# A two-layer hybrid trunk on one core: chunked linear attention with two-chunk scores, its steps placed by hand between projection matmuls

## The chip, the core and the metric

The kernel runs on one core of a Trainium2 chip. TensorE (PE in the profile) does the matmuls and writes PSUM, 8 banks of 128 partitions by 512 float32; VectorE (DVE), ScalarE (ACT) and GpSimd (POOL) do the rest, each in the order of its own instruction stream, and wait for one another by semaphores. DMA engines bring the weights. The metric is the device time of one execution, in microseconds (us). The kernel before took 851.46 us, the median of 3 runs (850.23 to 853.15).

## The reference

512 tokens of width 1024 go through two layers and a last RMSNorm. Each layer does a modulated RMSNorm, one input projection, two mixers side by side, a product with SiLU of a gate, an output projection and a gated residual. The change lies in the second layer, whose mixers are chunked gated linear attention (4 heads, keys of 128, values of 256, chunks of 64 tokens) and stick-breaking attention (8 heads of 128).

```python
def gla(q, k, v, log_a):
    ...
    bcum = jnp.cumsum(la, axis=2)
    b_last = bcum[:, :, -1]
    q_dec = qf * jnp.exp(bcum)
    k_inv = kf * jnp.exp(-bcum)
    k_end = kf * jnp.exp(b_last[:, :, None] - bcum)
    att = jnp.einsum('bnthk,bnshk->bnhts', q_dec, k_inv)
    att = jnp.where(mask, att, 0.0)
    o_intra = jnp.einsum('bnhts,bnshv->bnthv', att, vf)

    def step(state, xs):
        qd, ke, vc, bl = xs
        o = jnp.einsum('bthk,bhkv->bthv', qd, state)
        state = jnp.exp(bl)[..., None] * state + jnp.einsum('bshk,bshv->bhkv', ke, vc)
        return state, o
```

The outputs of a head are then normalised over their 256 values. Stick-breaking attention takes q, k and v of its own from the same projection.

## The kernel before

Everything is float32. A projection is exact to nearly float32: a weight tile is split into a high part (`whi`, ScalarE, L184) and the rest (`wlo`, VectorE, L185), both in the type fp32r, and three matmuls add up high by high, low by high and high by low (`mm3`, L198 to L200). `c_unit` makes 256 output channels for all 512 tokens in two PSUM banks; `t_unit` makes 512 channels with the tokens on the partitions, in four. These use 6 banks of the tag `mm`; everything small shares 2 banks of the tag `aux`. One weight tile feeds 24 projection matmuls and comes by one DMA of 512 KB on SyncE's queue; there are 4 buffers for raw tiles and 3 for split ones.

Of the second layer the order of the source is: the values of the linear attention (`gv`, two `t_unit`), the low-rank gate (`glr`, 16 matmuls, L564 and L565), and then for each of two pairs of heads `c`: `decay` of both heads (one matmul over 32 rows, L572, then logs, eight scans and exponentials on ScalarE and VectorE), the projections of k and q with their evacuation into decayed copies (`k_evac`, `q_evac`), and four steps `p`, each over two chunks of 64 (128 tokens). A step has four parts for both heads: scores (L638 and L639), output (L652 and L654), transposes of the decayed k (L661) and state update (L667, L671). For the scores the two chunks need different decays, so the first chunk is one matmul of 64 keys by 64 queries with `k1` (L638), and the second is one of 128 keys by 64 queries with `k2` (L639). ScalarE (L643) and VectorE (L644) copy them to `att`, and GpSimd (L645) puts zeros above the diagonal. After four steps come the norms (L684 and L685), then the two value projections `sv` of the stick-breaking attention, and then its 8 heads.

In this whole part a scheduler sets the order of each engine's instructions, TensorE's too. It is free to put small matmuls between any two projection matmuls. Only the stick-breaking heads stand under `manual_schedule`: there TensorE's order is that of the source, and `boundary`, called after each 12 projection matmuls (`quarter`), issues what `steps` holds for that gap (L715, L742 and L750).

Of the kernel before, what the change touches and what calls it, by code (L numbers as in the profile page):

```python
# [9 lines left out]
F32 = mybir.dt.float32  # L10
# [7 lines left out]
P = 128  # L18
# [21 lines left out]
def pack_inputs(i):  # L40
# [57 lines left out]
def trunk(ctx: ExitStack, tc: tile.TileContext, d, out):  # L98
# [447 lines left out]
    gv = [big("gv") for _ in range(TB)]  # L546
    t_unit(lambda kp: nxt(), 4, h_left(), tok_evac(gv, 0),
# [14 lines left out]
    ps = bank("aux")  # L562
    for k in range(KT):
        T.matmul(ps, gwv[:, k, :], h_hi[k], start=k == 0, stop=False)  # L564
        T.matmul(ps, gwv[:, k, :], h_lo[k], start=False, stop=k == KT - 1)  # L565
    glr = slot("silu")
    A.copy(out=glr[0:32], in_=ps[0:32])
# [27 lines left out]
    t_unit(lambda kp: nxt(), 4, h_left(), tok_evac(gv, 1))  # L595
# [5 lines left out]
    for c in range(2):  # L601
        dec = [decay(2 * c + j) for j in range(2)]
        k1, k2, k3, qd, qi = ([None, None] for _ in range(5))
# [29 lines left out]
        for p in range(TB):  # L633
# [14 lines left out]
            for j in range(2):  # L648
                for vt in range(2):
# [3 lines left out]
                    if p:  # L653
                        T.matmul(ov, st[j][:, vt * P:(vt + 1) * P], qi[j][:, r], start=False, stop=True)  # L654
# [208 lines left out]
```

## Time and profile before

| | |
|---|---|
| median of 3 runs | 851.46 us (850.23 to 853.15) |
| the profiled execution | 850.56 us |
| its span, first to last instruction | 848.8 us |
| busy: TensorE, VectorE, ScalarE, GpSimd | 97%, 60%, 47%, 8% of the span |
| mean granted TensorE clock | 0.995 of full speed |
| HBM read | 105.56 MB, 127 GB/s over the span |

The time of an execution is its span and some 2 us around it. Busy shares are averages over stages. A group of small float32 matmuls counts two records for each instruction. TensorE's records overlap, since a matmul drains while the next one streams, so the price of an instruction is the distance from its start to the next one's start and not its duration.

### The profile page before, as it was taken

The numbers are of one execution on the slowest core, as the hardware profiler recorded it, in microseconds if no ns is written. First come the engines' busy times: TensorE is split into PE (matmuls) and PEld (weight loads), VectorE is DVE, ScalarE is ACT, GpSimd is POOL, SyncE is SP. The second block draws the span as 40 slices with busy tenths as digits, with TensorE's granted clock in tenths as the row PEclk, the third lists the DMA queues.
The fourth block names the chain that finished last, engine by engine and source line by source line (L and its number), as shares of the span: only waits on it lengthen the run. The fifth ranks groups of instructions, "written<-read, shape, count | busy, mean of one in ns | idle before, by whom it ended". The sixth has DMA issues, their size and how long they took to land.

```text
span 848.8 us, 10038 instructions
## 1 busy us (share of the span) xinstructions
PE 825.2 (97%) x3720; PEld 661.3 (78%) x3720; DVE 511.0 (60%) x813; ACT 396.3 (47%) x663; POOL 65.8 (8%) x135
## 2 busy tenths in 40 slices
PE   5999999999999999999999999999999999989996
PEld 3778888888888887787877778877777777768884
DVE  6866655597773477642735643275657668433875
ACT  5463221233333366542425343365757678433553
POOL 2002111100000000000010200011010101020011
PEclk9999999999999999999999999999999999999998
DMA  8886555554552245423211202322121213232362
GB/s 287 291 293 220 178 170 174 199 178 160 180 181 89 84 151 187 133 78 100 98 51 50 75 29 96 100 82 92 61 89 46 83 47 100 79 95 87 115 218 78
DMA packets 31362, 108.31 MB, mean 128 GB/s; under 512 B 3633, under 2 KB 3761, under 8 KB 31314
## 3 DMA queue, kind: packets, MB, share of 16 engines
q1 hardware_dynamic: 30738, 106.63, 38.0%
q10 hardware_dynamic: 576, 1.05, 0.3%
q8 instruction: 29, 0.48, 0.2%
q14 instruction: 19, 0.16, 0.1%
HBM read 105.56 MB, written 2.10 MB: 127 GB/s over the span
## 4 chain that ended last, share of the span: by engine, by line
PE 88%; DVE 4%; DMA 3%; issue 1%; ACT 1%; POOL 1%; SPq 0%; POOLq 0%; ACTq 0%; DVEq 0%
PE mm L199 25%; PE mm L200 25%; PE mm L198 25%; PE aux L715 2%; PE aux L750 2%; DMA raw<-in_adaT 1%; DVE wlo L185 1%; PE aux L742 1%; DMA raw<-in_w 1%; DVE raw L174 1%; PE aux L652 1%; PE aux L464 1%; DMA x<-in_x 1%; PE aux L667 1%; PE aux L639 1%
## 5 line engine op out<-in xcount | busy, mean ns | idle before, releaser
L185 DVE TENSOR_TENSOR wlo<-raw,whi 128x1024 fp32r<-128x1024 f32 (+1 forms) x146 | 177.5, 1217 | 124.7 <-ACT whi L184 124.6
L184 ACT ACTIVATE whi<-raw 128x1024 fp32r<-128x1024 f32 (+1 forms) x146 | 152.6, 1045 | 195.2 <-PE mm L199 84.4
L198 PE MATMUL mm<-hhi,whi 128*128 128x512 f32 x576 | 233.1, 405 | 0.0
L200 PE MATMUL mm<-hhi,wlo 128*128 128x512 f32 x576 | 225.6, 392 | 0.0
L199 PE MATMUL mm<-hlo,whi 128*128 128x512 f32 x576 | 224.7, 390 | 0.0
L199 PEld LDWEIGHTS mm<-hlo,whi 128*128 128x128 f32 x576 | 108.3, 188 | 24.0 <-issue 2.7
L200 PEld LDWEIGHTS mm<-hhi,wlo 128*128 128x128 f32 x576 | 108.1, 188 | 23.7 <-issue 0.8
L198 PEld LDWEIGHTS mm<-hhi,whi 128*128 128x128 f32 x576 | 108.3, 188 | 23.2 <-issue 1.9
L174 DVE CUSTOM_DVE_ANT_0 raw<-raw,sc,cols 128x1024 f32<-128x1024 f32 x48 | 61.5, 1283 | 50.6 <-DMA raw<-in_adaT 50.5
L198 PE MATMUL mm<-whi,hhi 128*128 128x512 f32 x192 | 76.4, 400 | 0.4 <-ACT whi L184 0.2
L199 PE MATMUL mm<-wlo,hhi 128*128 128x512 f32 x192 | 76.4, 398 | 0.1
L200 PE MATMUL mm<-whi,hlo 128*128 128x512 f32 x192 | 74.7, 396 | 0.8 <-DVE hlo L319 0.8
L200 PE MATMUL mm<-whi,r 128*128 128x512 f32 x160 | 62.6, 391 | 0.0
L198 PE MATMUL mm<-whi,r 128*128 128x512 f32 x160 | 62.4, 391 | 0.0
L199 PE MATMUL mm<-wlo,r 128*128 128x512 f32 x160 | 62.4, 390 | 0.0
L200 PEld LDWEIGHTS mm<-whi,hlo 128*128 128x128 f32 x192 | 36.3, 189 | 8.8 <-DVE hlo L319 1.7
L198 PEld LDWEIGHTS mm<-whi,hhi 128*128 128x128 f32 x192 | 36.5, 191 | 8.3 <-ACT whi L184 0.6
L199 PEld LDWEIGHTS mm<-wlo,hhi 128*128 128x128 f32 x192 | 36.7, 191 | 7.8 <-DVE wlo L185 0.5
L190 DVE TENSOR_TENSOR r<-y,r 128x256 fp32r<-128x256 f32 (+1 forms) x60 | 29.1, 509 | 19.3 <-PE mm L199 16.1
L189 ACT ACTIVATE r<-y 128x256 fp32r<-128x256 f32 (+1 forms) x60 | 27.0, 479 | 29.2 <-PE mm L200 23.2
L199 PEld LDWEIGHTS mm<-wlo,r 128*128 128x128 f32 x160 | 30.0, 188 | 6.4 <-DVE wlo L185 0.3
L198 PEld LDWEIGHTS mm<-whi,r 128*128 128x128 f32 x160 | 30.0, 188 | 6.1
(186 smaller groups left out, 1043.9 us busy)
## 6 DMA issues: line engine op xcount, KB each, us to landing
raw<-in_w SPq DMA_DIRECT2D x90, 512.0 KB, 3.3
raw<-in_adaT SPq DMA_DIRECT2D x48, 512.0 KB, 4.1
raw<-in_wo SPq DMA_DIRECT2D x48, 512.0 KB, 3.3
raw<-in_wfirst SPq DMA_DIRECT2D x8, 384.0 KB, 4.3
x<-in_x SPq DMA_DIRECT2D x4, 512.0 KB, 5.2
kq<-in_poolw SPq DMA_DIRECT2D x4, 256.0 KB, 4.4
out<-x SPq DMA_DIRECT2D x4, 256.0 KB, 2.3
out<-x ACTq DMA_DIRECT2D x4, 256.0 KB, 2.6
```

Of the source, the lines that this page charges most:

```text
L174: V.tensor_tensor_reduce(out=t, in0=t, in1=sc, scale=1.0, scalar=cols[:, C_AB[l] + b:C_AB[l] + b + 1], op0=ALU.mult, op1=ALU.add, accum_ou ...
L184: A.activation(out=hi[:, :w], in_=t[:, :w], func=AF.Copy)
L185: V.tensor_tensor(out=lo[:, :w], in0=t[:, :w], in1=hi.bitcast(F32)[:, :w], op=ALU.subtract)
L189: A.activation(out=hi, in_=src, func=AF.Copy)
L190: V.tensor_tensor(out=lo, in0=src, in1=hi.bitcast(F32), op=ALU.subtract)
L198: T.matmul(o, lh, rh, start=start, stop=False)
L199: T.matmul(o, lh, rl, start=False, stop=False)
L200: T.matmul(o, ll, rh, start=False, stop=stop)
L464: T.matmul(ps[:, t * P:(t + 1) * P], v[t][:, hd * P:(hd + 1) * P], sguw[hd // 4][:, c], start=True, stop=True)
L639: T.matmul(ps[:, j * P + 64:(j + 1) * P], k2[j][:, r], qd[j][:, rb], start=True, stop=True)
L715: T.matmul(ps[:, c0:c0 + (t + 1) * P], q[:, t * P:(t + 1) * P], k[:, :(t + 1) * P], start=True, stop=True)
L750: T.matmul(ps[:, s * P:], sv[s][:, hd * P:(hd + 1) * P], wt[s], start=s == 0, stop=s == 3)
```

## The change

The scores of a step become one matmul for each head: 128 keys of both chunks by 192 columns, which are the queries of the first chunk, those of the second, and those of the second once more with the first chunk's decay in them. So `q_evac` writes a tile `qx` of 4 times 192 columns (GpSimd's copy L624 is gone), `k_evac` makes `k1` and `k3` from whole rows and no `k2`, and the transposes of k move into the same step as the scores. Of the 192 columns the copies to `att` take the first and third 64 for the first chunk's keys and the second 64 for the second chunk's keys.

TensorE's order is fixed from the second half of `gv` on. `at` and `boundary` now serve the linear attention too: `low_rank`, the four `decay`, and, for each pair of heads, the parts `scores`, `outputs` and `norm` are given gaps between 12 projection matmuls (`plan`, `decay_at`). Each pair of heads gets one of the two `sv` projections, whose gaps take its steps: the stream of weight tiles `w1` is now gv, gv, then k, q, sv for each pair. `nxt.deepen(1)`, which splits weight tiles one ahead, starts there. `gv` and `sv` are kept as halves, the first half of `sv` in slots of the tag `y`, and `kt` has two buffers.

```diff
     g1 = 5136
     s1 = [t_tiles(w1, 1024), t_tiles(w1, 1536)]
     for c in range(2):
-        s1 += [c_tiles(w1, 512 + 256 * c), c_tiles(w1, 256 * c)]
-    s1 += [t_tiles(w1, 4112), t_tiles(w1, 4624)]
+        s1 += [c_tiles(w1, 512 + 256 * c), c_tiles(w1, 256 * c), t_tiles(w1, 4112 + 512 * c)]
     for c in range(4):
         s1 += [c_tiles(w1, 2064 + 256 * c), c_tiles(w1, 3088 + 256 * c), c_tiles(w1, g1 + 256 * c)]
     s1 += [c_tiles(w1, g1 + 256 * c) for c in range(4, 8)]
...
     glr = slot("silu")
-    A.copy(out=glr[0:32], in_=ps[0:32])
+
+    def low_rank():
+        ps = bank("aux")
+        for k in range(KT):
+            T.matmul(ps, gwv[:, k, :], h_hi[k], start=k == 0, stop=False)
+            T.matmul(ps, gwv[:, k, :], h_lo[k], start=False, stop=k == KT - 1)
+        A.copy(out=glr[0:32], in_=ps[0:32])
...
+
+
+    steps, gap = {}, [0]
+
+    def at(g, f):
+        steps.setdefault(g, []).append(f)
+
+    def boundary():
+        for f in steps.pop(gap[0], []):
+            f()
+        gap[0] += 1
+
+    def c_steps(f):
+        c_unit(nxt, f, quarter=boundary)
+        boundary()
+
+    def t_steps(dst):
+        t_unit(lambda kp: nxt(), 4, h_left(), half_evac(dst),
+               groups=[e for kp in range(4) for e in (((0, 1), (kp,)), boundary, ((2, 3), (kp,)), boundary)])
+
...
+    def gla_pair(c):
+
+        k1, k3, qx, edec, st = ([None, None] for _ in range(5))
+        o, att, kt = [], {}, {}
 
         def k_evac(j, ps):
-            e, ei, kf = (half(t) for t in dec[j])
-            k1[j], k2[j], k3[j] = slot("kq"), slot("kq"), slot("kq")
-            a, b, z, q = half(k1[j]), half(k2[j]), half(k3[j]), half(ps)
-            V.tensor_tensor(out=a[:, :, 0], in0=q[:, :, 0], in1=ei[:, :, 0], op=ALU.mult)
-            V.tensor_tensor(out=z[:, :, 1], in0=q[:, :, 1], in1=kf[:, :, 1], op=ALU.mult)
-            V.tensor_tensor(out=b[:, :, 0], in0=q[:, :, 0], in1=kf[:, :, 0], op=ALU.mult)
-            V.tensor_tensor(out=b[:, :, 1], in0=q[:, :, 1], in1=ei[:, :, 1], op=ALU.mult)
-            V.tensor_tensor(out=z[:, :, 0], in0=b[:, :, 0], in1=e[:, :, 1, 63:64].to_broadcast([P, 4, 64]),
-                            op=ALU.mult)
-        c_unit(nxt, k_evac)
-        edec = [None, None]
+            e, ei, kf = dec[2 * c + j]
+            k1[j], k3[j] = slot("kq"), slot("kq")
+            V.tensor_tensor(out=k1[j], in0=ps, in1=ei, op=ALU.mult)
+            V.tensor_tensor(out=k3[j], in0=ps, in1=kf, op=ALU.mult)
+            z = half(k3[j])[:, :, 0]
+            V.tensor_tensor(out=z, in0=z, in1=half(e)[:, :, 1, 63:64].to_broadcast([P, 4, 64]), op=ALU.mult)
 
         def q_evac(j, ps):
-            e = half(dec[j][0])
-            qd[j], qi[j] = slot("r"), slot("r")
-            V.scalar_tensor_tensor(out=qd[j], in0=ps, scalar=GLA_DK ** -0.5, in1=dec[j][0], op0=ALU.mult,
+
+            e = half(dec[2 * c + j][0])
+            qx[j] = pool.tile([P, 768], F32, name=nm("qx"), tag="qx", bufs=2)
+            x = qx[j].rearrange("p (n b c) -> p n b c", b=3, c=64)
+            V.scalar_tensor_tensor(out=x[:, :, 0:2], in0=half(ps), scalar=GLA_DK ** -0.5, in1=e, op0=ALU.mult,
                                    op1=ALU.mult)
-            a, b = half(qd[j]), half(qi[j])
-            G.tensor_copy(out=b[:, :, 0], in_=a[:, :, 0])
-            V.tensor_tensor(out=b[:, :, 1], in0=a[:, :, 1], in1=e[:, :, 0, 63:64].to_broadcast([P, 4, 64]),
+            V.tensor_tensor(out=x[:, :, 2], in0=x[:, :, 1], in1=e[:, :, 0, 63:64].to_broadcast([P, 4, 64]),
                             op=ALU.mult)
             edec[j] = sm("edec", 4)
             V.tensor_tensor(out=edec[j], in0=e[:, :, 0, 63], in1=e[:, :, 1, 63], op=ALU.mult)
-        c_unit(nxt, q_evac)
-
-        o = [slot("y") for _ in range(4)]
-        st = [None, None]
-        for p in range(TB):
+
+        def scores(p):
             r = slice(p * P, (p + 1) * P)
             ps = bank("aux")
             for j in range(2):
-                ra, rb = slice(p * P, p * P + 64), slice(p * P + 64, (p + 1) * P)
-                T.matmul(ps[0:64, j * P:j * P + 64], k1[j][:, ra], qd[j][:, ra], start=True, stop=True)
-                T.matmul(ps[:, j * P + 64:(j + 1) * P], k2[j][:, r], qd[j][:, rb], start=True, stop=True)
-            att = atts[p % 2]
-            av = att.rearrange("p (j q) -> p j q", j=2)
-            pv = ps[:, :2 * P].rearrange("p (j q) -> p j q", j=2)
-            A.copy(out=av[0:64, :, 0:64], in_=pv[0:64, :, 0:64])
-            V.tensor_copy(out=av[:, :, 64:128], in_=pv[:, :, 64:128])
-            G.affine_select(out=att, in_=att, pattern=[[0, 2], [1, P]], compare_op=ALU.is_ge, fill=0.0, base=0,
+                T.matmul(ps[:, j * 192:(j + 1) * 192], k1[j][:, r], qx[j][:, p * 192:(p + 1) * 192], start=True,
+                         stop=True)
+            att[p] = atts[p % 2]
+            av = att[p].rearrange("p (j b c) -> p j b c", j=2, c=64)
+            pv = ps[:, :384].rearrange("p (j n c) -> p j n c", j=2, c=64)
+            A.copy(out=av[0:64], in_=pv[0:64, :, 0:3:2])
+            V.tensor_copy(out=av[64:128, :, 1], in_=pv[64:128, :, 1])
+            G.affine_select(out=att[p], in_=att[p], pattern=[[0, 2], [1, P]], compare_op=ALU.is_ge, fill=0.0, base=0,
                             channel_multiplier=-1)
+            if p == TB - 1:
+                return
             ps = bank("aux")
             for j in range(2):
+                T.transpose(ps[:, j * P:(j + 1) * P], k3[j][:, r], ident)
+            kt[p] = pool.tile([P, 2 * P], F32, name=nm("kt"), tag="kt", bufs=2)
+            V.tensor_copy(out=kt[p], in_=ps[:, :2 * P])
+
...
+        def plan(g):
+            for n, f, a in ((1, scores, 0), (2, scores, 1), (3, outputs, 0), (4, scores, 2), (5, outputs, 1),
+                            (6, scores, 3), (7, outputs, 2), (9, outputs, 3), (11, norm, 0), (14, norm, 1)):
+                at(g + n, lambda f=f, a=a: f(a))
+        return k_evac, q_evac, plan
+
+    def decay_at(g, hd):
+        def f():
+            dec[hd] = decay(hd)
+        at(g, f)
+
+    nxt.deepen(1)
+    order = ctx.enter_context(ExitStack())
+    order.enter_context(tc.manual_schedule(engines={T.engine}))
+    at(0, low_rank)
+    for hd, g in enumerate((3, 5, 14, 16)):
+        decay_at(g, hd)
+    gv[1] = halves("gv")
+    t_steps(gv[1])
+    sv = [None, None]
+    for c in range(2):
+        k_evac, q_evac, plan = gla_pair(c)
+        c_steps(k_evac)
+        c_steps(q_evac)
+        plan(gap[0])
+        sv[c] = halves("sv") if c else [slot("y") for _ in range(TB)]
+        t_steps(sv[c])
```

Left out are the evacuation of `gv` and `sv` into halves, `outputs`, `squares` and `norm`, which hold the same operations as before, and the loops of the stick-breaking heads, which call the same units at the same gaps.

Where TensorE's instructions stand, in the first pair of heads, third step. Before, the scores of that step follow the state update of the step before (L667), and six projection matmuls later comes the output that needs them (`aux_3485`):

```order
L667 MATMUL aux_3470<-gv_2860,kt_3468 128x256 x2
L638 MATMUL aux_3477<-r_3397,kq_3319 64x64
L639 MATMUL aux_3477<-r_3397,kq_3320 128x64
L638 MATMUL aux_3477<-r_3404,kq_3327 64x64
L639 MATMUL aux_3477<-r_3404,kq_3328 128x64
L200 MATMUL mm_3614<-hhi_121,wlo_3618 128x512
L198 MATMUL mm_3613<-hhi_122,whi_3647 128x512
L199 MATMUL mm_3613<-hlo_130,whi_3647 128x512
L200 MATMUL mm_3613<-hhi_122,wlo_3648 128x512
L198 MATMUL mm_3613<-hhi_123,whi_3647 128x512
L199 MATMUL mm_3613<-hlo_131,whi_3647 128x512
L652 MATMUL aux_3485<-att_3203,gv_2861 128x128
```

After, the same step's scores (`qx` is the tile of queries, `aux_3587` the scores) stand alone between 12 projection matmuls and 12 more, with the transposes of k behind them:

```order
L199 MATMUL mm_3439<-whi_3510,hlo_131 128x512
L660 MATMUL aux_3587<-qx_3424,kq_3327 128x192
L660 MATMUL aux_3587<-qx_3429,kq_3332 128x192
L673 MATMUL aux_3593<-ident,kq_3328 128x128
L673 MATMUL aux_3593<-ident,kq_3333 128x128
L197 MATMUL mm_3440<-whi_3510,hhi_122 128x512
L198 MATMUL mm_3440<-wlo_3511,hhi_122 128x512
```

The output that needs these scores stands 36 projection matmuls further on, behind the output and state update of the second step and the scores of the fourth; the state update has moved directly behind the output of its own step.

On VectorE, between the evacuation of the first pair's q and its part of the first scores. Before there is one weight split (`wlo`) between them:

```order
L621 SCALAR_TENSOR_TENSOR r_3397<-mm_3335,z_3225 128x512
L625 TENSOR_TENSOR r_3398<-r_3397,z_3225 128x4x64
L621 SCALAR_TENSOR_TENSOR r_3404<-mm_3336,z_3250 128x512
L625 TENSOR_TENSOR r_3405<-r_3404,z_3250 128x4x64
L185 TENSOR_TENSOR wlo_3696<-raw_3693,whi_3695 128x1024
L644 COPY att_3203<-aux_3415 128x2x64
```

After, the decays of the second pair of heads (L586, L589, L593 and L599; `misc_3391` is the first, `misc_3464` the second) stand among them, and the copy of the transposed k (`kt`) and the score copy (`att`) come behind these rows:

```order
L651 TENSOR_TENSOR qx_3424<-qx_3424,z_3169 128x4x64
L586 TENSOR_SCALAR misc_3391<-aux_3387,cols 128x512
L589 TENSOR_TENSOR misc_3391<-misc_3391,misc_3389 128x512
L593 SCALAR_TENSOR_TENSOR misc_3396<-ones,misc_3391 128x64 x8
L649 SCALAR_TENSOR_TENSOR qx_3429<-mm_3338,z_3224 128x4x128
L599 TENSOR_TENSOR sp_3407<-misc_3396 128x512
L651 TENSOR_TENSOR qx_3429<-qx_3429,z_3224 128x4x64
L184 TENSOR_TENSOR wlo_3511<-raw_3508,whi_3510 128x1024
L654 TENSOR_TENSOR edec_3872<-z_3405 128x4
L586 TENSOR_SCALAR misc_3464<-aux_3460,cols 128x512
L589 TENSOR_TENSOR misc_3464<-misc_3464,misc_3462 128x512
L593 SCALAR_TENSOR_TENSOR misc_3469<-ones,misc_3464 128x64 x8
```

The rows show that VectorE now has two decays to do between the end of the q projection and its part of the first scores, where it had none.

## Rows read from the trace of the kernel before

**Rows 1.** The page: busy time, share of the span and instruction records of each engine (part 1), and the share of each engine in the chain of work that ended last (part 4).

```profile
PE 825.2 (97%) x3720; PEld 661.3 (78%) x3720; DVE 511.0 (60%) x813; ACT 396.3 (47%) x663; POOL 65.8 (8%) x135
...
PE 88%; DVE 4%; DMA 3%; issue 1%; ACT 1%; POOL 1%; SPq 0%; POOLq 0%; ACTq 0%; DVEq 0%
```

**Rows 2.** Five stretches of the span (us from its start), with the busy time and the number of records of each engine in it, then TensorE's granted clock, the share of the DMA engines and GB/s. The first three hold the gated linear attention, the fourth the value projection of the stick-breaking attention, the fifth the stick-breaking attention up to its last projections.

```profile
424.00:450.00 26.00, 25.32 (x150) 19.80 (x149) 8.43 (x17) 5.47 (x18) 3.21 (x5) 1.00 0.15 48
450.00:476.00 26.00, 26.00 (x108) 19.11 (x108) 20.31 (x48) 17.35 (x30) 1.36 (x2) 1.00 0.12 41
476.00:500.00 24.00, 23.77 (x142) 18.86 (x142) 9.37 (x18) 5.35 (x18) 3.85 (x5) 1.00 0.20 66
500.00:552.10 52.10, 52.10 (x232) 42.60 (x231) 18.94 (x21) 20.09 (x31) 0.00 (x0) 1.00 0.28 91
552.10:742.00 189.90, 189.90 (x849) 149.54 (x848) 123.20 (x175) 128.00 (x222) 18.15 (x48) 1.00 0.23 75
```

**Rows 3.** The waits of TensorE from 375 to 553 us: who waited for whom, us in total, times, longest.

```profile
PE aux L652 <- POOL att L645: 0.9, 2, 0.7
```

**Rows 4.** TensorE's timeline in the first pair of heads, third chunk pair: start, us, engine, line, tiles, shapes, count of records. A plain float32 matmul leaves two records, an fp32r one leaves one; the durations overlap, so a cost is read from one start to the next. L667 is the state update, L638 and L639 are the scores, L652 begins the output, L198 to L200 are projection matmuls.

```profile
437.19 1.11 PE L667 MATMUL aux<-gv,kt 128*128 128x256 f32 x4
438.23 0.33 PE L638 MATMUL aux<-r,kq 128*64 128x64 f32 x2
438.49 0.43 PE L639 MATMUL aux<-r,kq 128*128 128x64 f32 x2
438.85 0.33 PE L638 MATMUL aux<-r,kq 128*64 128x64 f32 x2
439.11 0.43 PE L639 MATMUL aux<-r,kq 128*128 128x64 f32 x2
439.35 0.48 PE L200 MATMUL mm<-hhi,wlo 128*128 128x512 f32 x1
439.67 0.39 PE L198 MATMUL mm<-hhi,whi 128*128 128x512 f32 x1
...
440.59 0.40 PE L199 MATMUL mm<-hlo,whi 128*128 128x512 f32 x1
441.67 0.49 PE L652 MATMUL aux<-att,gv 128*128 128x128 f32 x2 [0.68 <-POOL att L645]
```

**Rows 5.** The chain that ended last, 434 to 442 us: start, us that the piece adds to the chain, what.

```profile
435.09 0.22 PE aux L652 x2
...
437.35 0.95 PE aux L667 x4
...
439.64 0.27 ACT att L643
...
439.93 0.30 DVE att L644
...
440.29 1.34 POOL att L645
```

**Rows 6.** TensorE's timeline in the stick-breaking attention, around one float32 score matmul of 256 moving columns (L715) between projection matmuls.

```profile
558.99 0.39 PE L200 MATMUL mm<-hhi,wlo 128*128 128x512 f32 x1
559.22 0.59 PE L715 MATMUL aux<-kq,kq 128*128 128x256 f32 x2
559.46 0.59 PE L198 MATMUL mm<-hhi,whi 128*128 128x512 f32 x1
559.88 0.40 PE L199 MATMUL mm<-hlo,whi 128*128 128x512 f32 x1
```

**Rows 7.** Groups of TensorE instructions from 375 to 553 us: line, tiles, shapes, count of records, then busy us and mean ns of one.

```profile
L639 PE MATMUL aux<-r,kq 128*128 128x64 f32 x32 | 6.9, 296 | 0.0
...
L638 PE MATMUL aux<-r,kq 128*64 128x64 f32 x32 | 5.3, 246 | 0.0
```

**Rows 8.** VectorE's timeline in the second pair of heads: L580, L584 (eight scans) and L590 belong to one decay, L577 to the next one, L621 is the evacuation of q, L613 a product over half the columns, L185 the split of a weight tile, L644 its part of the score copy.

```profile
464.11 0.68 DVE L580 TENSOR_TENSOR misc<-misc,misc 128x512 f32<-128x512 f32 x1
464.83 1.57 DVE L584 TENSOR_TENSOR_SCAN misc<-ones,misc 128x64 f32<-128x64 f32 x8
466.43 0.69 DVE L590 TENSOR_TENSOR sp<-misc 128x512 f32<-128x512 f32 x1
467.04 0.74 DVE L577 TENSOR_SCALAR misc<-aux,cols 128x512 f32<-128x512 f32 x1
...
468.03 0.68 DVE L621 SCALAR_TENSOR_TENSOR r<-mm,z 128x512 f32<-128x512 f32 x1
...
472.42 0.41 DVE L613 TENSOR_TENSOR kq<-kq,z 128x256 f32<-128x256 f32 x1
...
475.50 1.21 DVE L185 TENSOR_TENSOR wlo<-raw,whi 128x1024 fp32r<-128x1024 f32 x1
...
477.44 0.29 DVE L644 COPY att<-aux 128x128 f32<-128x128 f32 x1 [0.41 <-ACT att L643]
```

**Rows 9.** TensorE's timeline around one decay matmul (L572, 32 rows by 512 columns).

```profile
458.29 1.12 PE L572 MATMUL aux<-silu,silu 32*128 32x512 f32 x2
459.34 0.50 PE L199 MATMUL mm<-hlo,whi 128*128 128x512 f32 x1
```

**Rows 10.** The timeline of all engines: the split of the first weight tile of `gv`'s second half, and the first matmul of the low-rank gate (L564).

```profile
371.50 1.23 DVE L185 TENSOR_TENSOR wlo<-raw,whi 128x1024 fp32r<-128x1024 f32 x1 [1.78 <-ACT whi L184]
...
375.65 0.39 PE L564 MATMUL aux<-hhi,glr_w 128*128 128x512 f32 x1
```

More of the change, by code (lines that the diff above doesn't have):

```diff
@@ L545, in trunk, with halves, half_evac @@
     nxt = stream(d["w1"])
-    gv = [big("gv") for _ in range(TB)]
-    t_unit(lambda kp: nxt(), 4, h_left(), tok_evac(gv, 0),
+    def halves(n):
+        t = [big(n) for _ in range(2)]
+        return [t[i // 2][:, (i % 2) * 512:(i % 2 + 1) * 512] for i in range(TB)]
+    def half_evac(dst):
+        return lambda t, ps: (V.tensor_copy if t % 2 else A.copy)(out=dst[t], in_=ps)
+    gv = [halves("gv"), None]
+    t_unit(lambda kp: nxt(), 4, h_left(), half_evac(gv[0]),
            groups=(late, ((0, 1), (0, 1, 2)), ((2, 3), (0, 1, 2)), ((0, 1, 2, 3), (3,))))
@@ L649, in trunk, with outputs @@
+            V.tensor_copy(out=kt[p], in_=ps[:, :2 * P])
+        def outputs(p):
+            if not p:
+                o.extend(slot("y") for _ in range(4))
+            r = slice(p * P, (p + 1) * P)
+            ps = bank("aux")
+            for j in range(2):
+                x = qx[j].rearrange("p (n b c) -> p n b c", b=3, c=64)[:, p, 0:3:2]
                 for vt in range(2):
                     c0 = j * 256 + vt * P
-                    ov = ps[:, (2 * j + vt) * P:(2 * j + vt + 1) * P]
@@ L657, in trunk @@
             if p == TB - 1:
-                break
+                squares(0)
+                return
             ps = bank("aux")
             for j in range(2):
-                T.transpose(ps[:, j * P:(j + 1) * P], k3[j][:, r], ident)
-            kt = pool.tile([P, 2 * P], F32, name=nm("kt"), tag="kt", bufs=1)
-            V.tensor_copy(out=kt, in_=ps[:, :2 * P])
-            ps = bank("aux")
-            for j in range(2):
-                c0 = j * 256
-                T.matmul(ps[:, c0:c0 + 256], kt[:, j * P:(j + 1) * P], gv[p][:, 512 * c + c0:512 * c + c0 + 256], start=True, stop=True)
+                c0 = slice(j * 256, (j + 1) * 256)
+                T.matmul(ps[:, c0], kt[p][:, j * P:(j + 1) * P], gv[c][p][:, c0], start=True, stop=True)
             for j in range(2):
@@ L675, in trunk, with squares @@
                 st[j] = new
-        for j in range(2):
-            hd = 2 * c + j
+        held = {}
+        def squares(j):
             q0, q1 = slot("misc"), slot("misc")
@@ L749, in stick_out @@
         for s in (0, 1, 2, 3):
-            T.matmul(ps[:, s * P:], sv[s][:, hd * P:(hd + 1) * P], wt[s], start=s == 0, stop=s == 3)
+            T.matmul(ps[:, s * P:], sv[hd // 4][s][:, hd % 4 * P:(hd % 4 + 1) * P], wt[s], start=s == 0, stop=s == 3)
         y[8 + hd] = slot("y")
@@ L767, in trunk, with add_head @@
     q, k, last = {}, {}, []
[L768 to L770 removed]
+    def add_head(hd, g):
         block, wt = {}, {}
+        at(g + 12, lambda: last.append(stick_out(hd, wt)))
         for i in range(3):
[L773 to L775 removed]
+            at(g + i, lambda i=i: stick_weights(q[hd], k[hd], i, block))
+            at(g + 9 + i, lambda i=i: stick_turn(block, TURNS[i], wt))
+    g0 = gap[0]
     for c in range(4):
[L777 to L784 removed]
+        add_head(2 * c, g0 + 12 * c + 8)
+        add_head(2 * c + 1, g0 + 12 * c + 14)
     def sb_proj(dst, c, scale):
@@ L793, in gated, with multiply, evac @@
         return lambda j, ps: gate_exp(y[2 * c + j], ps)
[L795 to L823 removed]
+    for c in range(4):
+        for f in (sb_proj(q, c, SB_DH ** -0.5), sb_proj(k, c, 1.0), gated(c)):
+            c_steps(f)
+    held = []
+    for c in range(4, 8):
+        sg = [None, None]
+        def multiply(c=c, sg=sg):
+            for j in range(2):
+                t = y[2 * c + j]
+                G.tensor_tensor(out=t, in0=t, in1=sg[j], op=ALU.mult)
+        def evac(j, ps, sg=sg):
+            held.append((sg, j, ps))
+        if c < 6:
+            c_steps(gated(c))
+            continue
+        c_unit(nxt, evac, quarter=boundary)
+        held.append(multiply)
+        boundary()
+        if not steps:
+            for e in held:
+                if callable(e):
+                    e()
+                    continue
+                with tc.issue_after(last[-1].ins):
+                    silu_to(e[0])(e[1], e[2])
+            held.clear()
+    order.close()
     gbc = gate_rows(1)
```

64 lines of the change are left out of this document (10 added, 54 removed).

## The prediction

> **What bounds the kernel now.** I read the page first: TensorE is busy 97% of the span and holds 88% of the chain that ended last [rows 1], so the time is the length of TensorE's stream plus its holes. Then the busy time by stretch [rows 2]: the reader should look at the first two figures of each line. From 424 to 552 us, the linear attention and the projection after it, TensorE is idle for 0.68 + 0.23 us; from 552 to 742 us for nothing. TensorE's clock is granted in full (1.00, which is 2.4 GHz) in each of them, so no clock is to be won. VectorE is busy 20.31 of 26 us in the worst stretch, ScalarE 17.35, the DMA engines at most 28%: none of them is the bound, but VectorE can be late for a while. Third, the waits: in the whole stretch that changes TensorE waits twice, 0.9 us in all, for GpSimd's masking of the scores [rows 3]. So nearly all that the change can win must come out of TensorE's own instructions, and all that it can lose is a new hole. Fourth, TensorE's timeline, read from start to start, gives the price of these instructions [rows 4].
>
> **The change, part by part.** In order, the instructions of TensorE ahead of the low-rank gate and behind the first stick-breaking heads stand as before, and SyncE issues the same DMAs in the same order (the weights are packed in the new order of use). So I count only the stretch from 375 to 552 us.
>
> *The scores.* From the start of L667 at 437.19 to the second projection matmul at 439.67 are 2.48 us [rows 4]. In them are one projection matmul, 0.23 us (558.99 to 559.22), and two state matmuls of 256 columns; one float32 matmul of 256 columns between projection matmuls takes 559.22 to 559.88 less 0.23, that is 0.43 us [rows 6], two 0.87. What is left, 2.48 - 0.23 - 0.87 = 1.38 us, is four score matmuls and the small costs at the edges of the group. The edges are seen in the rows: L638 begins 1.04 us after L667, not 0.87, and the distances from L638 to L639 and back are 0.26 and 0.36 us for the same 64 columns, so each change between 64 and 128 keys costs something.
>
> After, two matmuls of 192 columns do this. No row shows one; the bounds are 128 columns, 0.22 us (L652 [rows 5]), and 256 columns, 0.43 us [rows 6]. I take the middle, 0.33, since the two bounds are nearly in the ratio of their columns; two are 0.66, with 0.44 and 0.86 as ends. All have full 128 by 128 weights, as the neighbours have, so there is no change of shape left. A step wins 1.38 - 0.66 = 0.72 us. There are 16 L638 and 16 L639 (32 records each, two for one [rows 7]), which is 8 steps, and I price the two first steps, which stand alone between projection matmuls, like the other six: 8 x 0.72 = 5.8 us, with ends of 8 x 0.52 = 4.2 and 8 x 0.94 = 7.5.
>
> The Trainium skill speaks against this: in "TensorE: Matmul & The Clock Gate", section "Back-to-back issue gap", the distance between matmuls grows with the moving columns alone, with the remark that weight loads add to it where columns are few. By columns alone the step goes from 256 to 384 columns and gets longer. The trace does not agree as far as four matmuls of 64 columns go, which take 1.38 us where four of 128 take 0.88 [rows 5].
>
> *The waits for the mask.* Before, the output L652 followed six projection matmuls after the scores, 1.4 us of cover, while the chain of ScalarE's copy, VectorE's copy and GpSimd's mask is 0.27 + 0.30 + 1.34 with hand-overs, 2.0 us [rows 5]. L652 started 1.08 us after the last projection matmul instead of 0.23 [rows 4]: 0.85 lost where the profile says 0.68. After, the output stands at least 24 projection matmuls (5.4 us) behind its scores, so both waits go. They are 0.9 us as idle time [rows 3], about 1.2 by starts; I take 1.0.
>
> *What the fixed order adds.* TensorE can no longer be given other work when a small part is late. What stands behind a waiting part is everything. There are 20 small groups in the new stretch (4 decays, 8 scores, 8 outputs) at gaps of 12 projection matmuls (2.7 us), and at most two `aux` banks change hands in a gap. I looked for the tightest place, the first pair's scores, since VectorE's stream there has two decays in it. Count from the end of the q projection. The first decay's matmul stands 2.7 us earlier, its logs are done by then; VectorE does eight scans 1.57, the second head's q 0.68, L590 0.69 and the product over half the columns 0.41 [rows 8], so q is ready after 3.4 us. The scores come after 24 projection matmuls and a decay (1.05 us, [rows 9]), at 6.5: 3 us to spare. The second scores come 2.7 + 1.1 us later, at 10.3, and need the bank from which VectorE copies its part of the first ones. Ahead of that copy VectorE has a weight split 1.21, the next decay 0.74 + 0.68 + 1.57 + 0.69, a copy of k of about 0.41 and the copy itself 0.29: 5.6 us, ready at 9.0, 1.3 us to spare. For the second pair no decay stands there. So I cost the new waits at nothing; if a handful of groups waits, 0 to 2 us.
>
> *What costs nothing.* `k_evac` goes from five products over half the columns to two over all and one over half (5 x 0.41 against 2 x 0.69 + 0.41, about 1.8 us for a head both times), the POOL copy goes, `qx` writes as many columns as before in two instructions. All this lies under TensorE's projection matmuls. The low-rank gate moves behind 12 of them, so the second half of `gv` begins where the gate began, at 375.65 us, 16 matmuls or 3.6 us earlier than before; its first weight tile was split by 371.50 + 1.23 = 372.7 [rows 10], in time for that. The next tile is needed 24 + 16 matmuls later, which is 9 us for a split. If that cover failed once, the low part would come one split, 1.2 us, late.
>
> Sum: 5.8 + 1.0 = 6.8 us. The profiled execution of before took 850.56 us, its span 848.8 and 1.8 around it, which is 0.9 under the median of the runs. From it 843.8; beside the median of 851.46 I predict 844.7 us.
>
> **The rivals.** *VectorE is late at the second pair's decays.* The spare 1.3 us assumes that VectorE's instructions follow each other without gaps, while they also wait for ScalarE's logs and exponentials. If both scores wait there for one split and the wait passes on to the first output, 3 x 1.2 us are given back: 844.7 + 3.6 = 848.3. For it: VectorE 20.31 of 26 us busy [rows 2]. Against it: the 5.4 us between parts.
>
> *The columns count.* If the 1.38 us are not the price of 64-column matmuls but of leaving the projection stream and coming back, that part stays. By columns the four took 4 x 0.11 = 0.45 us (half of 0.22) and the rest, 0.93, is the edge; after there is 0.66 + 0.93 = 1.59, and 8 x 0.21 = 1.7 us are lost against 1.0 from the waits: 852.2. Against it: the group of one 256-column matmul shows no edge [rows 6].
>
> *The two `aux` banks bind.* With the order fixed, each group must find its bank emptied, and ScalarE and VectorE empty it in their own order, often behind a split of 1.2 us. If each of 20 groups waits 0.85 us, the longest seen at a start [rows 4], that is 17 us: 861.7. It turns the sign once a group waits 0.34 us on average. Against it: two waits in the whole stretch before, with less distance between the parts.
>
> **How the numbers follow.** About 0.3% (2.5 us) is what a measurement can tell from no change. The forecast has 0.72: its own ends are 4.2 + 1.0 - 2 = 3.2 and 7.5 + 1.2 = 8.7 us, that is 842.8 to 848.3, all of it faster. VectorE late has 0.13, mostly still faster (under 848.9), 0.03 of it the same. Columns 0.08, the same. Banks 0.07, slower. So faster 0.82, same 0.11, slower 0.07. The range is 842.3 to 849.2: the forecast's ends, the first rival, and half a microsecond of the runs' spread at the low end.
>
> **What would show it.** Right: the small float32 matmuls of 192 columns about 0.33 us from start to start, no change of shape around them; no wait of the output for GpSimd; the first stick-breaking score matmul about 6.8 us earlier in the span and everything behind it shifted by the same. Wrong: in the waits of TensorE, scores waiting for VectorE's q or copies (the first rival) or any small group for ScalarE's or VectorE's emptying of a bank (the third), or 192 columns taking 0.43 us or more with an edge before them (the second).

## The result, and the profile after

The changed kernel takes 842.48 us, the median of four runs (840.86 to 843.82), beside 851.63 (850.23 to 853.15) for the kernel before: the ratio is 0.9896 [0.9879, 0.9914], about 9 us less.

The page after, to be read against [rows 1]: busy time of each engine, and the engines' shares of the chain that ended last.

```profile
PE 817.4 (97%) x3688; PEld 660.5 (79%) x3688; DVE 512.2 (61%) x805; ACT 396.7 (47%) x663; POOL 61.0 (7%) x131
...
PE 89%; DVE 4%; DMA 3%; ACT 1%; issue 1%; POOL 1%; SPq 0%; POOLq 0%; ACTq 0%; DVEq 0%
```

TensorE is the bound as before: 97% of a span that is now 839.0 us. Its own busy time went from 825.2 to 817.4 us, 32 records fewer (16 score matmuls of two records each), so most of the gain lies in its own instructions; of holes there were few to close.

To see where, I measure one stretch in every kernel: from the first matmul that follows the first half of `gv` (in the kernel before this is the low-rank gate, L564 [rows 10]) to the first score matmul of the stick-breaking heads, 512 columns wide. Its two ends stand in TensorE's timeline, of the kernel after here:

```profile
374.81 0.39 PE L197 MATMUL mm<-whi,hhi 128*128 128x512 f32 x1
```

and, 168.7 us on:

```profile
543.51 1.02 PE L776 MATMUL aux<-kq,kq 128*128 128x512 f32 x2
```

and its end in the kernel before here:

```profile
551.98 1.02 PE L715 MATMUL aux<-kq,kq 128*128 128x512 f32 x2
```

That is 551.98 - 375.65 = 176.33 us before and 543.51 - 374.81 = 168.7 after, 7.6 less. The whole program's difference is larger in these two profiled executions (9.8 us of span). The rest lies where no instruction of TensorE was moved: the stretch begins 0.84 earlier, which arose in the first 55 us, in waits for the first transfers and splits whose length differs from run to run (in the nine further profiles below it began between 375.1 and 381.1, in eight of them after one more wait near 209 us), 1.1 us lie in a stretch of halved clock behind the gate rows, which is taken up below, and 0.3 at the end.

The busy time after, columns as in [rows 2]: the whole stretch, and the 26 us of it in which VectorE is busiest.

```profile
374.81:543.51 168.70, 168.70 (x801) 139.18 (x800) 82.28 (x143) 68.16 (x121) 4.30 (x8) 1.00 0.23 78
411.00:437.00 26.00, 26.00 (x114) 20.06 (x113) 18.25 (x40) 12.08 (x18) 1.45 (x1) 1.00 0.24 82
```

And the busiest 26 us of VectorE before:

```profile
453.50:479.50 26.00, 25.77 (x108) 18.40 (x107) 22.02 (x50) 14.24 (x23) 3.99 (x3) 1.00 0.18 61
```

In the first two lines the first two figures are alike: TensorE has no idle time in the stretch, at full clock. VectorE is busy for 18.25 of its busiest 26 us, where it was 22.02 before: the decays are spread out. The two longest kinds of TensorE's waits on VectorE in the whole program, columns as in [rows 3]:

```profile
PE aux L307 <- DVE n L298: 3.3, 5, 1.7
PE aux L328 <- DVE rep L327: 3.1, 4, 0.9
```

None of TensorE's waits lies in the stretch (L307 is ahead of it, L328 is behind the stick-breaking heads); the wait for GpSimd's mask [rows 3] is gone, and no other came in its place.

TensorE's timeline around a score group (L660) and the start of an output group (L687) of the first pair, to be read from start to start against [rows 4]:

```profile
453.11 0.39 PE L199 MATMUL mm<-whi,hlo 128*128 128x512 f32 x1
453.33 0.81 PE L660 MATMUL aux<-qx,kq 128*128 128x192 f32 x4
453.85 0.53 PE L197 MATMUL mm<-whi,hhi 128*128 128x512 f32 x1
454.21 0.40 PE L198 MATMUL mm<-wlo,hhi 128*128 128x512 f32 x1
...
456.52 0.39 PE L199 MATMUL mm<-whi,hlo 128*128 128x512 f32 x1
456.75 0.38 PE L687 MATMUL aux<-att,gv 128*128 128x128 f32 x2
```

From the start of the scores to the second projection matmul behind them are 454.21 - 453.33 = 0.88 us; less one projection matmul (0.23) leave 0.65 for two matmuls of 192 columns, 0.325 each. The output L687 follows its projection matmul at 0.23, where L652 followed at 1.08 [rows 4].

### The profile page after: what moved, and what is told of

Read it like the earlier page. It is cut to its first block, busy times and chain, and to the rows that moved or that the text cites. A ratio compares the mean times of both kernels' runs of the same rounds, so it can differ in the third digit from the quotient of the medians.

```text
span 839.0 us, 9962 instructions
## 1 busy us (share of the span) xinstructions
PE 817.4 (97%) x3688; PEld 660.5 (79%) x3688; DVE 512.2 (61%) x805; ACT 396.7 (47%) x663; POOL 61.0 (7%) x131
## 4 chain that ended last, share of the span: by engine, by line
PE 89%; DVE 4%; DMA 3%; ACT 1%; issue 1%; POOL 1%; SPq 0%; POOLq 0%; ACTq 0%; DVEq 0%
PE mm L198 26%; PE mm L199 26%; PE mm L197 25%; PE aux L776 2%; PE aux L811 2%; DVE wlo L184 1%; DMA raw<-in_wfirst 1%; PE aux L803 1%; DVE raw L173 1%; DMA raw<-in_w 1%; PE aux L463 1%; PE aux L687 1%; DMA x<-in_x 1%; ACT whi L183 1%; PE aux L689 1%
## 5 line engine op out<-in xcount | busy, mean ns | idle before, releaser
L184 DVE TENSOR_TENSOR wlo<-raw,whi 128x1024 fp32r<-128x1024 f32 (+1 forms) x146 | 177.5, 1218 | 123.6 <-ACT whi L183 123.5
L198 PE MATMUL mm<-hlo,whi 128*128 128x512 f32 x576 | 224.5, 390 | 0.0
L198 PEld LDWEIGHTS mm<-hlo,whi 128*128 128x128 f32 x576 | 108.3, 188 | 23.1 <-issue 1.9
L197 PE MATMUL mm<-whi,hhi 128*128 128x512 f32 x192 | 78.2, 410 | 0.2 <-DVE hhi L317 0.2
L198 PE MATMUL mm<-wlo,hhi 128*128 128x512 f32 x192 | 76.2, 397 | 0.1
L198 PE MATMUL mm<-wlo,r 128*128 128x512 f32 x160 | 62.4, 390 | 0.0
L198 PEld LDWEIGHTS mm<-wlo,hhi 128*128 128x128 f32 x192 | 36.7, 191 | 7.5 <-DVE wlo L184 0.5
L188 ACT ACTIVATE r<-y 128x256 fp32r<-128x256 f32 (+1 forms) x60 | 27.0, 479 | 29.2 <-PE mm L199 23.2
L198 PEld LDWEIGHTS mm<-wlo,r 128*128 128x128 f32 x160 | 30.0, 188 | 6.4 <-DVE wlo L184 0.3
```

Source lines behind the costliest of these rows:

```text
L184: V.tensor_tensor(out=lo[:, :w], in0=t[:, :w], in1=hi.bitcast(F32)[:, :w], op=ALU.subtract)
L188: A.activation(out=hi, in_=src, func=AF.Copy)
L197: T.matmul(o, lh, rh, start=start, stop=False)
L198: T.matmul(o, lh, rl, start=False, stop=False)
```

## The experiments

Each run's stretch is given beside its time, since the stretch repeats far better than the run: two copies of unchanged kernels gave it again.

**The two kernels again** (`before_again`, `after_again`). No edit.

> The kernel before once more. The stretch from the low-rank gate to the first stick-breaking score should be 176.3 us again, with about 0.9 us of waits for the mask. If the loss of clock behind the gate rows (0.50 from 752 to 754 us) is chance, it may be missing here, and then the span is about 1.1 us shorter.

> The changed kernel once more, for its own spread. If the 0.85 us before the stretch and the 1.4 us behind it in the two profiled executions are chance (DMA arrivals at the start, the clock after the gate rows), the stretch is 168.7 us again, and the rest moves by about 1 us either way; if they belong to the change, they are there again.

Before: stretch 176.31 us, median 851.6 us, ratio 0.9997 [0.9975, 1.002]. After: stretch 168.71, median 842.81, ratio 0.9902 [0.9873, 0.993]. Each stretch came back within 0.02 us. So differences of a few tenths in the stretch can be read as effects of an edit, while the medians can't tell less than some 2 us. Outside the stretch two executions of one kernel differ far more: in the two profiles of the changed kernel the stretch begins at 374.81 and at 377.64, and what stands behind it takes 295.4 and 297.8 us. Four of the six runs of `after_again` lie between 842.39 and 842.90, two at 846.06 and 847.95.

**Old scores in the new place** (`old_scores`). The changed kernel, with the scores of before:

```diff
-T.matmul(ps[:, j*192:(j+1)*192], k1[j][:, r], qx[j][:, p*192:(p+1)*192], ...)
+T.matmul(ps[0:64, j*P:j*P+64], k1[j][:, ra], qx[j][:, x0:x0+64], ...)
+T.matmul(ps[:, j*P+64:(j+1)*P], k2[j][:, r], qx[j][:, x0+64:x0+128], ...)
```

> The changed kernel with the scores of before: per head one matmul of 64 keys by 64 queries and one of 128 keys by 64 queries, k2 made again, everything at the same gaps. If the form of the score matmuls pays (their edges and 64-column price, 1.31 us a step against 0.65), the stretch from the first matmul of gv's second half to the first stick-breaking score grows by 8 x 0.66 = 5.3 us, from 168.7 to 174.0, and the time goes from 842.5 to about 847.8. If the win came from the places of the steps, it stays within 1 us: 842.5 to 843.5.

The stretch is 173.56 us, 4.85 more than after; median 850.31, ratio 0.9981 [0.9962, 1.0001]. TensorE's timeline of one score group (L664 with 64 keys, L665 with 128, L677 transposes k):

```profile
434.66 0.39 PE L199 MATMUL mm<-whi,hlo 128*128 128x512 f32 x1
434.98 0.33 PE L664 MATMUL aux<-qx,kq 128*64 128x64 f32 x2
435.23 0.43 PE L665 MATMUL aux<-qx,kq 128*128 128x64 f32 x2
435.60 0.33 PE L664 MATMUL aux<-qx,kq 128*64 128x64 f32 x2
435.86 0.43 PE L665 MATMUL aux<-qx,kq 128*128 128x64 f32 x2
436.13 0.39 PE L677 MATMUL aux<-ident,kq 128*128 128x128 f32 x2
...
436.59 0.39 PE L198 MATMUL mm<-wlo,hhi 128*128 128x512 f32 x1
```

The group is entered after 0.32 us instead of 0.23, the distances inside it are 0.25 to 0.27 and 0.37. By the stretch the scores' form alone is worth 4.85 us of the 7.6, and the place the other 2.77. The medians say more for the form: on this chip (the runs of `after_again`, `full_keys_64` and `before_192` are of the same one) `old_scores` lies 7.5 us above the changed kernel. All medians there lie further above that of the changed kernel than their stretches do, by 0.9 to 2.7 us, perhaps because its median fell among its four low runs; I go by the stretch.

**Four matmuls of 64 columns, all with 128 keys** (`full_keys_64`). As the last, but no matmul has 64 keys any more; the rows that are not needed are not read.

```diff
-T.matmul(ps[0:64, j*P:j*P+64], k1[j][:, ra], qx[j][:, x0:x0+64], ...)
+T.matmul(ps[:, j*P:j*P+64], k1[j][:, r], qx[j][:, x0:x0+64], ...)
```

> As old_scores, but the first chunk's matmul takes all 128 keys too (the rows that are not needed are not read), so no matmul has a shape of its own: four matmuls of 128 keys by 64 columns a step. If the loading of weights bounds a matmul of 64 columns (0.107 us for each of two records), a step is 0.86 us, 0.2 more than with 192 columns: 8 x 0.2 = 1.7, 844.2. If 64 columns cost what they did before whatever the shapes (about 1.3), 847.8. If columns alone count (0.45), 840.9. The difference to old_scores is the price of the change of shape: 3.6, 0 or 7 us.

The stretch is 170.31 us, median 846.05, ratio 0.993 [0.9904, 0.9955]. The same group there:

```profile
434.60 0.39 PE L199 MATMUL mm<-whi,hlo 128*128 128x512 f32 x1
434.83 0.33 PE L664 MATMUL aux<-qx,kq 128*128 128x64 f32 x2
435.00 0.39 PE L665 MATMUL aux<-qx,kq 128*128 128x64 f32 x2
435.22 0.39 PE L664 MATMUL aux<-qx,kq 128*128 128x64 f32 x2
435.44 0.39 PE L665 MATMUL aux<-qx,kq 128*128 128x64 f32 x2
435.67 0.39 PE L677 MATMUL aux<-ident,kq 128*128 128x128 f32 x2
...
436.13 0.39 PE L198 MATMUL mm<-wlo,hhi 128*128 128x512 f32 x1
```

The entry is back at 0.23 and the steady distance is 0.22, for 64 columns as for the 128 of L652 [rows 5]. So the 4.85 us split: 173.56 - 170.31 = 3.25 are the change between 64 and 128 keys, and 170.31 - 168.71 = 1.60 are four short matmuls instead of two longer ones. A matmul of 64 keys is not slow in itself: in `old_scores` its two records start at 434.98 and 435.08, no further apart than any two records of a matmul of 128 columns (0.11).

**New scores in the old place** (`before_192`). The kernel before with `qx`, the new `k_evac` and the 192-column scores, and nothing moved.

> The kernel before with one score matmul of 192 columns per head and nothing else moved: the steps follow one another and the scheduler puts projection matmuls between them, six between scores and output as before. If the form of the scores is worth 5.3 us by itself, 851.6 becomes 846.3, and TensorE still waits for GpSimd's mask before some outputs, 1 to 2 us in all. If the places are what pays, 851 or, by columns, up to 853.

The stretch is 172.22 us, 4.11 less than before; median 847.45, ratio 0.9941 [0.9915, 0.9967]. The waits of its TensorE in the stretch, columns as in [rows 3]:

```profile
PE aux L647 <- POOL att L640: 1.0, 1, 1.0
```

The wait for the mask stays where the outputs stay, and it is larger than this line shows: each of the eight outputs starts 0.05 us after its mask's end, and the eight entries to an output sum to 3.79 us from start to start, beside 1.83 in the changed kernel. Of the two ways round, the form gives 4.1 to 4.85 us and the place 2.8 to 3.5. The two overlap. Behind the state update the first 192-column matmul begins 0.96 us after the update's start here (437.16 to 438.12), and the 64-key one 1.04 before [rows 4], where two matmuls of 256 columns are 0.87 [rows 6]: an entry behind that update costs something in either form.

**The output directly behind its scores** (`same_gap`). The changed kernel with each pair's four output parts in the gap of their scores; order of everything else as it was.

```diff
-((1, scores, 0), (2, scores, 1), (3, outputs, 0), (4, scores, 2), ...
+((1, scores, 0), (1, outputs, 0), (3, scores, 1), (3, outputs, 1), ...
```

> The changed kernel with each step's output directly behind its scores, in the same gap between projection matmuls. The chain of copies and mask takes about 2.0 us and only the transposes (0.4 us) lie beside it: each of 8 steps waits some 1.6 us, 13 us in all, about 855; if TensorE's clock falls in these holes, more. If an order that is fixed were enough by itself, 842.5.

The stretch is 197.95 us, median 875.62 of two runs, ratio 1.0276 [1.0219, 1.0333]: slower than the kernel before. The waits of its TensorE, and two windows (busy time of PE, PEld, DVE, ACT, POOL, then the granted clock):

```profile
PE aux L687 <- POOL att L667: 20.9, 8, 3.5
```

```profile
440.00:455.00 15.00, 9.24 (x49) 7.92 (x50) 5.81 (x13) 4.00 (x10) 1.86 (x2) 1.00 0.16 46
455.00:459.00 4.00, 4.00 (x17) 3.55 (x16) 0.29 (x1) 0.77 (x4) 0.00 (x0) 0.57 0.23 93
```

Each of eight outputs waits, 2.6 us on average; I had expected 1.6. VectorE's copy begins 2.5 to 2.7 us after the scores here, where it began 1.7 after them in [rows 4] and [rows 5] (438.23 to 439.93): in seven of the eight steps a weight split stands just ahead of it, in the first the decay. The waits bring a second cost: TensorE is busy for 9.24 of 15 us, and then its clock is granted at the lower level (0.57 over the next 4 us). It stood at 0.50 for 3.4 us four times in the stretch; each costs at most half of that, 1.7, so up to 6.8 us beside the 20.9 of idle time, which is 27.7 of the 29.2 that the stretch lost. The waits on TensorE cost more than their length here.

**One gap between scores and output** (`next_gap`). 12 projection matmuls as cover in place of 24 or more.

```diff
-((1, scores, 0), (2, scores, 1), (3, outputs, 0), (4, scores, 2), (5, outputs, 1), ...
+((1, scores, 0), (2, outputs, 0), (3, scores, 1), (4, outputs, 1), (5, scores, 2), ...
```

> The changed kernel with each output one gap behind its scores: 12 projection matmuls, 2.7 us, over a chain of 2.0. If only the chain has to be covered, 842.5, or up to 1.5 more where a weight split stands ahead of the copies. If the two small banks bind, waits of 0.3 us and more in most groups: over 847.

The stretch is 169.89 us, 1.18 more; median 846.23, ratio 0.9925 [0.9897, 0.9953]. One output of eight waits, the very first, and the timeline of all engines shows for what:

```profile
432.79 0.81 PE L660 MATMUL aux<-qx,kq 128*128 128x192 f32 x4
...
435.48 0.29 DVE L666 COPY att<-aux 64x128 f32<-64x128 f32 x1
...
435.81 1.23 DVE L184 TENSOR_TENSOR wlo<-raw,whi 128x1024 fp32r<-128x1024 f32 x1
435.85 1.45 POOL L667 TENSOR_SCALAR_AFFINE_SELECT att<-att 128x256 f32<-128x256 f32 x1 [67.67 <-DVE att L666]
...
437.36 0.82 PE L687 MATMUL aux<-att,gv 128*128 128x128 f32 x5 [0.78 <-POOL att L667]
```

VectorE's copy for the mask (L666) begins 2.69 us after the scores, behind the fourth decay (L593 to L599), and then GpSimd's mask (L667) takes 1.45 us beside VectorE's split of a weight tile (L184). In the other seven steps the copy is as late, 2.55 to 2.65 us after the scores, behind a split; but there the mask runs alone, takes 0.41 us, and ends 0.10 to 0.21 us before its output begins. What makes the first one wait is the slow mask.

**The same, with the fourth decay nine gaps later** (`next_gap_late_decay`).

```diff
-for hd, g in enumerate((3, 5, 14, 16)):
+for hd, g in enumerate((3, 5, 14, 25)):
```

> next_gap with the fourth decay moved from the gap ahead of the first scores to one behind the last output of the first pair of heads. next_gap waited once, 0.8 us, for the mask of the first scores, and its stretch was 169.89 us against 168.71. If VectorE's and ScalarE's work for that decay made the score copies late, the wait goes and the stretch is 168.7 to 168.9. If 12 projection matmuls are too little cover for the first scores whatever stands there, the wait stays and the stretch is 169.8 or more.

The stretch is 168.85 us, and TensorE has no wait left in it. One run, 846.02 us, beside 850.4 for the kernel before on the same chip; its time says little, but the stretch answers the question. The mask there:

```profile
433.67 0.81 PE L660 MATMUL aux<-qx,kq 128*128 128x192 f32 x4
...
435.08 1.22 DVE L184 TENSOR_TENSOR wlo<-raw,whi 128x1024 fp32r<-128x1024 f32 x1
...
436.32 0.29 DVE L666 COPY att<-aux 64x128 f32<-64x128 f32 x1
...
436.69 0.41 POOL L667 TENSOR_SCALAR_AFFINE_SELECT att<-att 128x256 f32<-128x256 f32 x1 [66.35 <-DVE att L666]
...
437.30 1.05 PE L687 MATMUL aux<-att,gv 128*128 128x128 f32 x8
```

The copy begins 2.65 us after the scores, nearly as late as with the decay in its old place; but it now comes behind the split, so the mask runs alone, takes 0.41 us and ends 0.20 before the output. The stretch is the one that I expected if the decay had made the copies late, and the reason is another: the decay only decided whether the split ran ahead of the copy or beside the mask. One gap is cover enough, by 0.1 to 0.2 us, while the mask runs alone; the second gap hides the slow mask in the changed kernel.

**The gate rows of the second layer earlier** (`early_gates`). Not a question of the prediction, but of the part behind it: in all kernels so far TensorE stops behind the stick-breaking heads for the rows L328. Here their two halves stand in two gaps ahead of the first stick-breaking head.

```diff
+    at(g0 + 4, lambda: rows.append(gate_rows(1, None, (0,))))
+    at(g0 + 5, lambda: gate_rows(1, rows[0], (1,)))
...
-    gbc = gate_rows(1)
+    gbc = rows[0]
```

> The changed kernel with the eight gate-row transposes of the second layer moved from the end of the attention to two gaps ahead of the stick-breaking heads. In the changed kernel TensorE waits 3.1 us there for VectorE's tiles, which take 1.2 us each beside GpSimd's products, and starts a few matmuls in between, 738.8 to 743.6 us. If these tiles are the cause, 3.5 to 4.5 us go, 838 to 839, and the clock has no reason to fall there. If the output projection waits for GpSimd's products of the last gate tiles anyway (4.9 us), at most 1 us goes: 841.5.

Median 838.93 of four runs (836.9 to 840.9), ratio 0.9845 [0.9811, 0.988]: lower than both kernels (the changed one had 0.9896 and 0.9902). The stretch has 169.68 us, with the moved transposes in it, 0.97 more; from the first matmul of the following projection to the end it takes 95.66 us instead of 100.15. Two windows around that place, after first and then this kernel:

```profile
739.50:743.50 4.00, 1.19 (x4) 0.53 (x4) 4.00 (x5) 1.95 (x4) 3.91 (x4) 1.00 0.00 0
```

```profile
739.00:742.00 3.00, 3.00 (x14) 2.45 (x14) 0.56 (x1) 2.97 (x5) 0.41 (x1) 1.00 0.00 0
```

TensorE is busy for 1.19 of 4 us there after, and without a break in this kernel, where the next projection's first matmul starts at 741.57. What held it was VectorE beside GpSimd; of the kernel after, all engines:

```profile
738.47 4.94 POOL L858 TENSOR_TENSOR y<-y,silu 128x512 f32<-128x512 f32 x4 [26.64 <-ACT silu L378]
738.76 4.74 DVE L327 TENSOR_SCALAR rep<-ones,ada 128x128 f32<-128x128 f32 x4 [2.32 <-PE aux L328]
```

Four small rows (L327, 128 by 128) take 4.74 us on VectorE while GpSimd multiplies (L858); alone one of them took 0.29 (at 369.43 in the kernel before), and in `early_gates` the moved ones take 0.28 each, with nothing on GpSimd beside them.

## Why the prediction was right

The forecast was a gain of 6.8 us in the stretch; it is 7.6. Step by step:

- *The scores, 5.8 us.* Right, with a part of it in the wrong place. Priced as the prediction priced them (from the last projection matmul ahead of a group to the second one behind it, less projection matmuls, state updates and transposes), the eight steps cost 11.1 us before and 5.2 after: 5.9. The form alone is worth less: taken out of the changed kernel 4.85, put into the old one 4.11, within the ends of 4.2 to 7.5 or just under. The price of 192 columns was right: 0.325 us measured, 0.33 taken. The old price of 1.38 us [rows 4] held a part that belongs to the place behind the state update and not to the form, 0.09 us in each of six steps by `before_192` (0.96 less 0.87). And in the changed kernel, with transposes behind the scores, `old_scores` loses 1.93 - 1.32 = 0.61 a step (434.66 to 436.59 there, 432.26 to 433.58 after, both with the transposes), not 0.72.
- *The waits for the mask, 1.0 us.* The term was too small. The eight entries from a projection matmul to an output sum to 3.19 us from start to start before and 1.83 after: 1.36, near the 1.2 that I read and didn't take. And the chain of 2.0 us that it rests on is the slow case: both masks that were waited for ran beside a weight split (1.33 us at 440.29, 1.32 at 477.81), the other six took 0.41. The place gave more than these waits, 2.77 us in all. In the sums of distances 0.28 of it is found inside the outputs (24 distances from L652 to L654, 5.61 against 5.33) and 0.57 in the normalisation's small matmuls, which now stand in pairs. The remainder, about half a microsecond, is a sum of edges: the six entries behind the state update give 0.5, the four decays, two of which stood side by side before, cost some 0.4 more, and no run takes the rest apart.
- *New waits, nothing.* Right: no line of TensorE's waits lies in the stretch. The spare time was near what I worked out, as the timeline after shows:

```profile
428.56 0.42 DVE L651 TENSOR_TENSOR qx<-qx,z 128x256 f32<-128x256 f32 x1
...
432.49 0.81 PE L660 MATMUL aux<-qx,kq 128*128 128x192 f32 x4
...
435.18 0.29 DVE L666 COPY att<-aux 64x128 f32<-64x128 f32 x1
...
435.51 1.23 DVE L184 TENSOR_TENSOR wlo<-raw,whi 128x1024 fp32r<-128x1024 f32 x1
435.55 1.45 POOL L667 TENSOR_SCALAR_AFFINE_SELECT att<-att 128x256 f32<-128x256 f32 x1 [67.67 <-DVE att L666]
...
436.12 0.81 PE L660 MATMUL aux<-qx,kq 128*128 128x192 f32 x4
...
438.00 0.41 POOL L667 TENSOR_SCALAR_AFFINE_SELECT att<-att 128x256 f32<-128x256 f32 x1 [1.00 <-DVE att L666]
...
439.75 1.05 PE L687 MATMUL aux<-att,gv 128*128 128x128 f32 x8
```

q is ready at 428.56 + 0.42 = 428.98, the scores L660 begin at 432.49: 3.5 us to spare, 3 predicted. VectorE's copy of the first scores ends at 435.47, and the second ones begin at 436.12: 0.65, where I had worked out 1.3. The mask runs beside a split, takes 1.45 and ends at 437.00, and its output begins at 439.75: 2.75 to spare.
- *No cost of the evacuations and the gate.* Nothing in the stretch speaks against it: a part that was late would show as a wait.
- *From 6.8 to the time.* By the medians the change is worth 9.2 us, and 8.5 in the second comparison, whose interval reaches from 6.0 to 10.8; by the stretch it is 7.6. Whether the rest is more than the runs' spread stays open. The median of 842.48 lies 2.2 under the forecast, under its own low end of 842.8, and 0.2 above that of the range, which had half a microsecond added for spread: that it lies inside is in part luck. The mechanism rests on the stretch.

*VectorE is late* did not come as it was told: VectorE's copy of the first scores was later than worked out, but no score waited for a copy in any version with the new order. The one wait of `next_gap`, 0.8 us for one output, came from the mask that ran beside a split. *The columns count* is refuted by the two runs on the form: 64 columns cost what 128 do, and the 0.36 us distances are changes between 64 and 128 keys. The Trainium skill's rule that spoke against the change ("TensorE: Matmul & The Clock Gate", section "Back-to-back issue gap") has the remark that weight loads add where columns are few. The trace goes the way of the remark and not of the columns alone: 0.22 us at 64 and at 128 columns, 0.325 at 192. That it is the weight loads which hold the 64 columns at 0.22, no run shows by itself. *The two banks bind* did not come: there is no wait for a bank in the stretch of any version with the new order, in `same_gap` neither, whose waits are all for the mask.

That the order is written out by hand is not shown to matter in itself: `same_gap` has a fixed order too and loses 29 us, and no run leaves the order to the scheduler with the steps called at these gaps.

## What to carry to other kernels

Where small matmuls stand in a stream that keeps TensorE full, count them by number and by shape before columns: here a matmul of 128 columns cost no more than one of 64, and two sizes of weights side by side cost on every change. Give a chain over several engines enough distance on the engine that bounds, and test how much: none cost 29 us, one gap was enough but for the one mask that ran beside a weight split, and two covered that one too. When a wait goes with an edit, read which link of the chain became shorter: here it was the mask, and not the copy that the edit was meant to hasten. Measure the effect in the stretch that changes, where it repeats within hundredths, and not only in the whole time.

## What the runs showed of the hardware

- GpSimd's mask of 128 by 256 takes 0.41 us alone and 1.32 to 1.46 beside VectorE's split of a weight tile (435.55 and 438.00 above; before at 440.29 [rows 5]). That holds without an exception for the 88 masks of the eleven profiles, of which 12 ran beside a split. VectorE's small rows L327 suffer in turn beside GpSimd's products, 1.07 to 1.30 us instead of 0.29. The Trainium skill ("GPSIMD Engine Reference", section "1. Specifications") has GpSimd share its memory interfaces with VectorE, with contention where VectorE reads two inputs; the split reads two tiles, and the trace agrees: the mask takes over three times as long.
- A change of the stationary operand between 64 and 128 columns cost 0.03 to 0.15 us each time: 0.32 for 0.23 at the entry, 0.25 to 0.27 for 0.22 on the way to 128 columns, 0.37 on the way back (the rows of `old_scores` and `full_keys_64`).
- The clock behind the gate rows falls in some executions and not in others. The windows of the kernel before, and of the changed kernel's second profile:

```profile
748.00:752.00 4.00, 1.33 (x4) 0.53 (x4) 4.00 (x5) 1.91 (x4) 3.88 (x4) 0.88 0.00 0
752.00:754.00 2.00, 1.98 (x5) 1.60 (x6) 1.10 (x1) 1.11 (x2) 0.00 (x0) 0.50 0.00 0
```

```profile
744.50:749.00 4.50, 3.51 (x9) 2.53 (x10) 2.97 (x3) 1.53 (x3) 1.75 (x2) 0.51 0.12 15
```

TensorE was busy for 1.33 of 4 us and then had half its clock (0.50, 1.2 GHz) for 3.4 us; in `after_again` for 6.8. In the first profile of after it did nearly the same, 1.19 of 4, and kept the full clock. In ten profiles with this hole the clock fell in eight, and not in the first of after and in `before_192`; what decides isn't shown. In `early_gates`, where the hole is filled, it didn't fall, but one profile can't tell that from chance.
